# The first MLP product's tile pool, claimed in another order, so that the pieces of w_up lie over the turned input of the convolution and attention's last outputs

## The chip, the cores and the metric

The kernel runs on one core of one Trainium2 chip. The metric is the time on the device in microseconds (us): one launch computes the whole layer. TensorE is called PE, its weight loads PEld, VectorE DVE, ScalarE ACT, GpSimd POOL and SyncE SP, as in the profile. SP does no arithmetic here: it issues most of the DMAs, in one queue, in the order of the program.

## The reference

One layer of a hybrid decoder trunk, for 2048 positions of width 1024, everything in float32:

```python
h = rms_norm(x, attn_norm_g)
z = h @ w_in                                  # q, k, v, gate_b, gate_c, xc
y_attn = swa_sink_attention(q, k, v, sinks)   # window 128, 8 heads of 64, 2 kv heads
y_conv = gate_b * short_conv(gate_c * xc, conv_w)
y = concat(rms_norm(y_attn, attn_out_g), rms_norm(y_conv, conv_out_g))
x = x + y @ w_out
hm = rms_norm(x, mlp_norm_g)
x = x + square(relu(hm @ w_up)) @ w_down      # w_up 1024 x 4096, w_down 4096 x 1024
```

## The kernel before, in words

**Three products for one.** Every float32 operand is split into a high and a low part of a shorter kind, and each product is made as three matmuls of 128x512: high by high, high by low, low by high. The split is two instructions: ACT casts the high part (L397 for blocks of x and of w_down, L416 for pieces of w_up), DVE subtracts it from the original to get the low part (L398, L417). The two products of the MLP are also done with seven block products in the place of eight, numbered 1 to 7; so operands are sums of blocks, and each block product `p` has its own x operand and its own w operand.

**Stages.** The positions go in four chunks of 512 through the mixers (attention and convolution, with the output projection). The last thing that the mixers do is the second half of the last chunk's output projection: matmuls into tiles `pout` from attention's outputs `at` and the weights `w_wo01`, a sum into the row tiles `x1` on DVE (L906), and a store of each of the four row tiles to `x1_dram`, issued by POOL (L913). The matmuls of the MLP's first product (tile `u`, L1421) begin in between: the operands of product 1 are made early (`wu_first0` to `wu_first3`), the others by the MLP's own code. The second product (tile `d`, L1528) comes at the end.

**The first product's loop.** `seq` lists (column group `n`, product `p`). At the start it is product 1 of groups 0 to 3, product 2 of groups 0 to 3, then products 6, 5, 7 of groups 0 to 2, then 3 and 4. Some steps ahead of its matmuls each operand is fetched: a piece of w_up is a tile of 128x512 in tag `w` (names `wu0_12` for group 0, block row 1, column 2; loaded by SP, L411), with 17 buffers; it is split into one of four `wop` tiles (L416 on ACT, L417 on DVE). The x operands `op_x0_p_0` and `op_x0_p_1` are loaded by SP from scratch in DRAM (L396) and split in place (L397, L398). Sums of pieces are made on DVE (L1136 to L1143). Beside the matmuls, `prepare_rest` brings the last 512 rows of x back from `x1_dram` in four tiles `xt_m3_0` to `xt_m3_3` (SP, L1219), and takes their squares on ACT (L275).

**What sets the order.** The code names the engine of every instruction; the framework's scheduler orders the instructions of each engine from the order of the code, priorities and its own costs, and adds the semaphore waits. A tile pool is a stretch of the on-chip memory SBUF; inside it every tag gets its place in the order in which the tags are first used. The MLP's pool opens where the mixers' pool was closed, at the same address, with waits by tile: whoever first writes a new tile waits for the last use of just those old tiles that lie under it. The few `memset` instructions on POOL of one column, with names that end in `_first`, write a first tile of a tag and so claim its place.

The mixers' pool holds, from its start: the row tiles `z` (0 to 12 KB per partition), two buffers `raw` (12 to 28 KB; in the last chunk they hold weights of the output projection, `w_wo11` and then `w_wo01`), five buffers `at` (28 to 48 KB, attention's outputs), `h0` (48 to 64 KB) and `h1` (64 to 80 KB). The last two hold the turned, normed input of the chunk, which the convolution's and the attention's projections read, and after that the blocks of x for the MLP (`xm0`, `xm1`) on their way to DRAM.

## Time and profile before

| | |
|---|---|
| time, median of 3 runs (lowest, highest) | 1934.71 us (1933.54, 1935.15) |
| the profiled execution's own time | 1934.5 us |
| its span, first to last instruction | 1932.8 us |
| PE busy | 1913.2 us, 99% of the span |
| DVE, ACT, POOL busy | 62%, 43%, 14% |
| DMA, mean over the span | 214 GB/s |
| first MLP product (u) | 2688 matmuls, 611.7 us busy |
| second MLP product (d) | 2688 matmuls, 609.4 us busy |

A PE that is busy for 99% of the span leaves some 20 us of gaps in all. Whatever is done on other engines shows in the time only where it opens or closes one of those gaps, or changes the clock that PE is granted.

### The profile page before, as it was taken

To read this page: it belongs to the slowest core of one execution; us is meant where nothing else is said; L and a number is where in the kernel's file an instruction comes from. 1 tells how busy PE (TensorE), PEld (TensorE's weight loads), DVE (VectorE), ACT (ScalarE), POOL (GpSimd) and SP (SyncE) were. 2 spreads that over 40 slices of the span, in tenths; PEclk is the share of its full clock that TensorE was granted. 3 is DMA by queue.
4 is the path that set the end of the run, shared out by engine and by line. 5 is a ranking of instruction groups with operands and counts; after the bars stand their busy time and mean duration, and the time that the engine had idled before them with its cause. 6 is when DMAs were issued, how large, how long until landed. Compare 5 with 4: busy or idle time off the path is not lost.

```text
span 1932.8 us, 24559 instructions
## 1 busy us (share of the span) xinstructions
PE 1913.2 (99%) x8923; PEld 1589.5 (82%) x8923; DVE 1204.1 (62%) x1848; ACT 830.8 (43%) x1565; POOL 275.9 (14%) x474
## 2 busy tenths in 40 slices
PE   8999999999999989999999999999999999999999
PEld 7888888888888778888888888888888888888887
DVE  4886657447456768989877766766534334448541
ACT  5564435335344437444565554554422233232320
POOL 1122212302221112223201110101000000100000
PEclk9999999999999999999999999999999999999999
DMA  9884854464463888777665544537964457766631
GB/s 295 321 306 135 312 211 175 187 249 153 193 267 140 264 282 283 232 235 245 209 233 195 181 162 138 169 124 294 378 211 152 142 164 228 264 228 223 206 135 55
DMA packets 232792, 414.32 MB, mean 214 GB/s; under 512 B 51672, under 2 KB 136160, under 8 KB 219872
## 3 DMA queue, kind: packets, MB, share of 16 engines
q1 hardware_dynamic: 203840, 336.98, 51.8%
q0 software_dynamic: 15424, 51.40, 6.8%
q10 hardware_dynamic: 13408, 24.39, 3.3%
q8 instruction: 70, 1.15, 0.2%
q14 instruction: 50, 0.41, 0.1%
HBM read 286.87 MB, written 125.83 MB: 214 GB/s over the span
## 4 chain that ended last, share of the span: by engine, by line
PE 93%; DMA 2%; DVE 2%; issue 1%; POOL 1%; ACT 1%; SPq 0%; ACTq 0%; POOLq 0%; DVEq 0%
PE d L1528 32%; PE u L1421 31%; PE pout L266 2%; PE pout L268 2%; PE pout L267 2%; PE pz L266 2%; PE pz L267 2%; PE pz L268 2%; PE psc_b L679 2%; PE pc_c L266 2%; PE px_c L266 2%; PE px_c L267 2%; PE pc_c L267 2%; PE pc_c L268 2%; PE px_c L268 2%; PE pb_c L267 1%
## 5 line engine op out<-in xcount | busy, mean ns | idle before, releaser
L1421 PE MATMUL u<-op_x,wop 128*128 128x512 f32 x2688 | 611.7, 390 | 4.6 <-ACT wop L416 4.6
L1528 PE MATMUL d<-op_w,op_f 128*128 128x512 f32 x2688 | 609.4, 389 | 0.0
L1421 PEld LDWEIGHTS u<-op_x,wop 128*128 128x128 f32 x2688 | 505.4, 188 | 110.3 <-ACT wop L416 5.2
L1528 PEld LDWEIGHTS d<-op_w,op_f 128*128 128x128 f32 x2688 | 504.5, 188 | 104.8
L398 DVE TENSOR_TENSOR op_f<-op_f 128x1024 fp32r<-128x1024 f32 x112 | 136.9, 1225 | 234.0 <-ACT op_f L397 233.6
L397 ACT CAST op_f<-op_f 128x1024 fp32r<-128x1024 f32 x112 | 117.5, 1050 | 353.3 <-DMA op_f<-fop 350.2
L416 ACT CAST wop<-wu 128x512 fp32r<-128x512 f32 x156 | 96.2, 620 | 89.9 <-PE u L1421 82.4
L417 DVE TENSOR_TENSOR wop<-wu,wop 128x512 fp32r<-128x512 f32 x156 | 110.6, 710 | 32.6 <-ACT wop L416 17.3
L1157 POOL DMA_DIRECT2D fop<-s x96 | 52.2, 543 | 440.5 <-DVE s L1160 436.3
L1163 DVE TENSOR_TENSOR u<-u,u 128x512 f32<-128x512 f32 x128 | 87.7, 685 | 22.1 <-PE u L1421 22.0
L398 DVE TENSOR_TENSOR op_w<-raw,op_w 128x1024 fp32r<-128x1024 f32 x56 | 68.4, 1222 | 26.3 <-ACT op_w L397 26.2
L397 ACT CAST op_w<-raw 128x1024 fp32r<-128x1024 f32 x56 | 58.8, 1053 | 44.9 <-PE d L1528 22.6
L1169 ACT ACTIVATE u<-u 128x512 f32<-128x512 f32 x64 | 40.5, 632 | 62.9 <-DVE u L1163 61.0
L696 ACT ACTIVATE sc_b<-sc_b,ngm_b 128x128 f32<-128x128 f32 x128 | 49.6, 389 | 25.6 <-DVE ngm_b L693 25.6
L728 POOL TENSOR_SCALAR_AFFINE_SELECT pp_b<-pp_b 128x512 fp32r<-128x512 f32 x60 | 39.8, 675 | 112.8 <-ACT pp_b L721 59.2
L1370 POOL DMA_DIRECT2D wds<-raw x16 | 8.6, 536 | 328.1 <-DVE raw L1368 328.1
L416 ACT CAST wop<-wu_s 128x512 fp32r<-128x512 f32 x64 | 39.6, 620 | 32.2 <-PE u L1421 26.1
L417 DVE TENSOR_TENSOR wop<-wu_s,wop 128x512 fp32r<-128x512 f32 x64 | 45.0, 702 | 12.4 <-ACT wop L416 12.1
L266 PE MATMUL pout<-w_wo,yt_c 128*128 128x512 f32 x128 | 52.5, 410 | 0.0
L268 PE MATMUL pout<-w_wo,yt_c 128*128 128x512 f32 x128 | 52.1, 407 | 0.0
L267 PE MATMUL pout<-w_wo,yt_c 128*128 128x512 f32 x128 | 51.2, 400 | 0.0
L266 PE MATMUL pout<-w_wo,at_b 128*128 128x512 f32 x128 | 50.2, 395 | 0.0
(256 smaller groups left out, 3109.4 us busy)
## 6 DMA issues: line engine op xcount, KB each, us to landing
op_f<-fop SPq DMA_DIRECT2D x112, 512.0 KB, 4.3
raw<-in_w_down_dram SPq DMA_DIRECT2D x72, 512.0 KB, 4.3
wu<-in_w_up_dram SPq DMA_DIRECT2D x128, 256.0 KB, 4.1
w_wo<-wo SPq DMA_DIRECT2D x24, 1024.0 KB, 6.8
fop<-s POOLq DMA_DIRECT2D x96, 256.0 KB, 2.5
fop<-u ACTq DMA_DIRECT2D x64, 256.0 KB, 2.9
op_x<-xop SPq DMA_DIRECT2D x28, 512.0 KB, 6.4
w_q<-q SPq DMA_DIRECT2D x12, 1024.0 KB, 6.2
```

What stands on the lines that cost most here:

```text
L266: nc.tensor.matmul(ps, st(0), mv(0), start=first, stop=False)
L267: nc.tensor.matmul(ps, st(0), mv(1), start=False, stop=False)
L268: nc.tensor.matmul(ps, st(1), mv(0), start=False, stop=last)
L397: nc.scalar.copy(op[:, 0], raw)
L398: nc.vector.tensor_tensor(op[:, 1], raw, op[:, 0].bitcast(F32), op=ALU.subtract)
L416: splits.append(nc.scalar.copy(hi, blk).ins)
L417: nc.vector.tensor_tensor(lo, blk, hi.bitcast(F32), op=ALU.subtract)
L696: nc.scalar.activation(sc[:, hd, :], sc[:, hd, :], AF.Exp, bias=ngm[:, hd : hd + 1], accum_out=den[:, hd : hd + 1])
L1157: eng.dma_start(fop_dram[tb][ORDER_DOWN.index(i)][n // 2][:, n % 2], b)
L1163: return nc.vector.tensor_tensor(dst, ps, b, op=ALU.add).ins
L1421: nc.tensor.matmul(pt, wops[i][:, a, k, :], xops[tb, p][k // 2][:, b, k % 2, :], start=p not in GOES_ON and k + j == 0, stop=k + j == NB + ...
L1528: nc.tensor.matmul(ps[tb][j], fs[tb][:, a, k, j * P : (j + 1) * P], w[:, b, k, :], start=first and p not in GOES_ON and k + n == 0, stop=l ...
```

## The change

```diff
-    for tag in ("f12", "s1", "s2", "s4", "u4", "f11", "w"):
+    for tag in ("u2", "f11", "f12", "s1", "s2", "s4", "u4", "st"):
         nc.gpsimd.memset(piece(tag, f"{tag}_first")[:, :1], 0.0)
+    nc.gpsimd.memset(pool.tile([P, D], F32, tag="xt", name="xt_m_first", bufs=2)[:, :1], 0.0)
+    nc.gpsimd.memset(piece("w", "w_first")[:, :1], 0.0)
```

No tile changes its size or its number of buffers. The order of the claims changes, and with it the place of each tag, counted from the pool's start in KB per partition:

| place | mixers' tile that lies there | MLP's tags before | MLP's tags after |
|---|---|---|---|
| 0 to 12 | z | f12, s1, s2, s4, part of u4 | u2, f11, part of f12 |
| 12 to 28 | raw (w_wo01, the projection's last weights) | u4, f11, 5 of the w | f12, s1, s2, s4, u4, 2 of the st |
| 28 to 48 | at (attention's last outputs) | 10 of the w | 3 of the st, xt, 3 of the w |
| 48 to 64 | h0 | 2 of the w, u2, 3 of the st | 8 of the w |
| 64 to 80 | h1 | 2 of the st, xt | 6 of the w |

So 14 of the 17 pieces of w_up now lie over `h0` and `h1`, where 15 lay over `raw` and `at`; the tiles `xt` for the last rows of x lie over `at`, where they lay over `h1`. Of the 13 pieces that SP loads first, 12 now take places of `h0` and `h1`; the thirteenth, `wu1_12`, lies over the fifth buffer of `at`, which the last chunk no longer uses.

The order of PE's, ACT's and DVE's instructions stays as it was. POOL gets three more memsets, and SP's queue changes in two places. The first is on SP at the end of the mixers, from the last weights of the output projection on. In brackets stand the semaphores that a DMA waits for: PE_49 and the like are counts of an engine's instructions, DMASW counts the landings of POOL's DMAs, DMAHW those of earlier DMAs. Before:

```order
L235 DMA w_wo013_1_6733<-wo01_1_2240 128x2048 [waits DMAHW1_49]
L396 DMA op_x0_2_0_6821<-xop0_1_77 128x1024 [waits DMAHW2_49,PE_49]
L396 DMA op_x0_2_1_6825<-xop0_1_77 128x1024 [waits DMAHW3_49,PE_49]
L1219 DMA xt_m3_0_7369<-x1_dram_75 128x1024 [waits DMAHW4_49,DMASW1_49]
L396 DMA op_x0_6_0_6829<-xop0_2_78 128x1024 [waits DMAHW5_49,Pool_49]
L396 DMA op_x0_6_1_6833<-xop0_2_78 128x1024 [waits DMAHW7_49,DMAHW6_49,DVE_49]
L411 DMA wu0_12_6839<-in_w_up_dram 128x4x128
L411 DMA wu1_12_6841<-in_w_up_dram 128x4x128 [waits DMAHW1_49,DMAHW0_49,PE_49]
L411 DMA wu2_12_6843<-in_w_up_dram 128x4x128
L411 DMA wu3_12_6845<-in_w_up_dram 128x4x128 [waits DMAHW2_49]
```

Now:

```order
L235 DMA w_wo013_1_6733<-wo01_1_2240 128x2048 [waits DMAHW1_49]
L396 DMA op_x0_2_0_6827<-xop0_1_77 128x1024 [waits DMAHW2_49,PE_49]
L396 DMA op_x0_2_1_6831<-xop0_1_77 128x1024 [waits DMAHW3_49,PE_49]
L396 DMA op_x0_6_0_6835<-xop0_2_78 128x1024 [waits DMAHW4_49,Pool_49]
L396 DMA op_x0_6_1_6839<-xop0_2_78 128x1024 [waits DMAHW5_49]
L411 DMA wu0_12_6845<-in_w_up_dram 128x4x128 [waits DMAHW6_49]
L411 DMA wu1_12_6847<-in_w_up_dram 128x4x128 [waits DMAHW7_49]
L411 DMA wu2_12_6849<-in_w_up_dram 128x4x128 [waits DMAHW0_49]
L411 DMA wu3_12_6851<-in_w_up_dram 128x4x128 [waits DMAHW1_49]
```

The load of `xt_m3_0`, which waits for the landing of POOL's first store to `x1_dram` (DMASW1), has left this place, and the wait of `wu1_12` for PE is gone; that one was for the last L267 of the output projection, into `pout3_0_1_3`. A second wait for PE further on, of `wu2_22` for the projection's very last matmul, is gone as well. The wait of `op_x0_6_0` for POOL stays; it is for the last mask of attention.

The second place is on SP too, some 25 loads later, where the pieces for groups 3 and 4 are loaded as earlier ones become free. Before:

```order
L411 DMA wu4_11_7230<-in_w_up_dram 128x4x128 [waits DMAHW7_49,DVE_49]
L1219 DMA xt_m3_1_7393<-x1_dram_75 128x1024 [waits DMAHW0_49]
L411 DMA wu4_21_7282<-in_w_up_dram 128x4x128 [waits DMAHW1_49,DVE_49]
L411 DMA wu4_22_7284<-in_w_up_dram 128x4x128 [waits DMAHW2_49,DVE_49]
L1219 DMA xt_m3_2_7422<-x1_dram_75 128x1024 [waits DMAHW3_49,Activation_49]
```

Now:

```order
L411 DMA wu4_11_7236<-in_w_up_dram 128x4x128 [waits DMAHW6_49,DVE_49]
L1221 DMA xt_m3_0_7375<-x1_dram_75 128x1024 [waits DMAHW7_49,PE_49]
L411 DMA wu4_21_7288<-in_w_up_dram 128x4x128 [waits DMAHW0_49,DVE_49]
L1221 DMA xt_m3_1_7399<-x1_dram_75 128x1024 [waits DMAHW1_49,PE_49]
L411 DMA wu4_22_7290<-in_w_up_dram 128x4x128 [waits DMAHW2_49,DVE_49]
L1221 DMA xt_m3_2_7428<-x1_dram_75 128x1024 [waits DMAHW7_49,DMAHW3_49,Activation_49]
```

`xt_m3_0` comes in here, and `xt_m3_1` falls back behind `wu4_21`, which waits for DVE to have made the low part of product 7 of group 0 (`wop_0_7`). Their waits for PE are for matmuls of the output projection.

On POOL the memsets stand behind the four stores of `x1`, as they did. Before:

```order
L913 DMA x1_dram_75<-x1_3_3_6228 128x1024
L1105 MEMSET f12_first_6805 128x1
L1105 MEMSET s1_first_6807 128x1
L1105 MEMSET s2_first_6809 128x1
L1105 MEMSET s4_first_6811 128x1
L1105 MEMSET u4_first_6813 128x1
L1105 MEMSET f11_first_6815 128x1
L1105 MEMSET w_first_6817 128x1
L1394 MEMSET op_first_6819 128x1
```

Now:

```order
L913 DMA x1_dram_75<-x1_3_3_6228 128x1024
L1105 MEMSET u2_first_6805 128x1
L1105 MEMSET f11_first_6807 128x1
L1105 MEMSET f12_first_6809 128x1
L1105 MEMSET s1_first_6811 128x1
L1105 MEMSET s2_first_6813 128x1
L1105 MEMSET s4_first_6815 128x1
L1105 MEMSET u4_first_6817 128x1
L1105 MEMSET st_first_6819 128x1
L1106 MEMSET xt_m_first_6821 128x1
L1107 MEMSET w_first_6823 128x1
L1396 MEMSET op_first_6825 128x1
```

Where the first product hands over to the second, the pool of the second lies over the first's, and a few waits change: the loads of w_down into `raw` (L1359) wait for the last splits of pieces of w_up, where they waited for the last stores of `u2` and of `wds`.

## The prediction

> **What bounds the kernel now.** I read the page first, then PE's waits, then the time around the one long wait, engine by engine. On the page, three lines:

> ```profile
> PE 1913.2 (99%) x8923; PEld 1589.5 (82%) x8923; DVE 1204.1 (62%) x1848; ACT 830.8 (43%) x1565; POOL 275.9 (14%) x474
> PE   8999999999999989999999999999999999999999
> L1421 PE MATMUL u<-op_x,wop 128*128 128x512 f32 x2688 | 611.7, 390 | 4.6 <-ACT wop L416 4.6
> L1528 PE MATMUL d<-op_w,op_f 128*128 128x512 f32 x2688 | 609.4, 389 | 0.0
> ```

> PE is the bound in all 40 slices; only the first slice and the fifteenth (676 to 725 us) are an 8. A change of layout cannot make matmuls fewer, so it can only touch gaps. The second MLP product has no idle time at all, the first has 4.6 us, all before one instruction, and the list of PE's waits has it at the top:

> ```profile
> PE u L1421 <- ACT wop L416: 4.6, 1, 4.6
> ```

> The timeline of PE shows its place; the rows of the table of windows below it have the window and its length, PE's busy time and matmuls, the granted clock, the DMA share and GB/s:

> ```profile
> 709.47 5.15 PE L1421 MATMUL u<-op_x,wop 128*128 128x512 f32 x22
> 719.20 41.04 PE L1421 MATMUL u<-op_x,wop 128*128 128x512 f32 x173 [4.58 <-ACT wop L416]
> 714.70:719.20 4.50, 0.01 (x1) 0.99 1.08 377
> 719.20:724.00 4.80, 4.80 (x14) 0.66 1.15 345
> 724.00:729.00 5.00, 5.00 (x23) 1.00 1.10 357
> ```

> PE ends product 1 of the first groups at 714.62, stands for 4.58 us, and then runs its next 4.8 us at a mean clock of 0.66. The change lies on this spot.

> **What holds the operand up.** PE waits for `wop_0_2`. The timelines of SP, ACT and DVE tell why it is late:

> ```profile
> 689.79 0.97 SPq L235 DMA_DIRECT2D w_wo<-wo  x2
> 692.66 0.80 SPq L396 DMA_DIRECT2D op_x<-xop  x2
> 706.05 0.32 SPq L1219 DMA_DIRECT2D xt_m<-x_dram  x1
> 706.46 0.86 SPq L396 DMA_DIRECT2D op_x<-xop  x2
> 707.37 16.64 SPq L411 DMA_DIRECT2D wu<-in_w_up_dram  x13
> 703.02 0.64 POOL L913 DMA_DIRECT2D x_dram<-x  x1 [7.89 <-DVE x L906]
> 713.70 1.05 ACT L397 CAST op_x<-op_x 128x1024 fp32r<-128x1024 f32 x1 [10.32 <-DMA op_x<-xop]
> 718.52 1.27 ACT L416 CAST wop<-wu 128x512 fp32r<-128x512 f32 x2 [1.46 <-DMA wu<-in_w_up_dram]
> 709.67 0.75 DVE L906 SCALAR_TENSOR_TENSOR x<-pout,ra,x 128x512 f32<-128x512 f32 x1 [1.97 <-PE pout L268]
> 714.78 1.23 DVE L398 TENSOR_TENSOR op_x<-op_x 128x1024 fp32r<-128x1024 f32 x1 [4.36 <-ACT op_x L397]
> 719.17 1.35 DVE L417 TENSOR_TENSOR wop<-wu,wop 128x512 fp32r<-128x512 f32 x2 [0.85 <-ACT wop L416]
> ```

> From 693.46 to 706.05, 12.6 us, SP's queue issues nothing: at its head stands `xt_m3_0`, which waits for POOL's store of 703.02 to land. Behind it stand `op_x0_6` and all 13 pieces of w_up. Then `wu1_12` waits once more, for the output projection's end. ACT gets `op_x0_6_0` at 713.70 and `wu0_12` at 718.52. DMA was not the limit while SP stood:

> ```profile
> 695.00:700.00 5.00, 5.00 (x24) 4.14 (x23) 0.75 (x1) 0.00 (x0) 0.13 (x1) 1.00 0.96 353
> 700.00:705.00 5.00, 5.00 (x24) 4.14 (x23) 3.04 (x4) 3.08 (x4) 0.64 (x1) 1.00 0.20 80
> ```

> The last column falls from 353 GB/s to 80 there, against 377 in the stall.

> **The change, part by part.** *Removed: both waits at the head of SP's queue.* `op_x0_6` now waits only for a mask of attention, which was made before the projection's last half, so it follows `op_x0_2` at 693.46 (13.0 us earlier), and `wu0_12` after another 0.86 us at 694.3. When do they land? The nearest rows are the DMA answers for the same two loads before (last column: us to landing, first for `op_x0_6_0`, then for `wu0_12`), and the longest landing of an x operand between 690 and 745 us:

> ```profile
> op_x<-xop SPq DMA_DIRECT2D x1, 512.0 KB, 7.2
> wu<-in_w_up_dram SPq DMA_DIRECT2D x1, 256.0 KB, 11.1
> DMA to landing us min/median/max: 5.8/8.5/12.9
> ```

> So `op_x0_6_0` lands at 700.7, at most 706.4; `wu0_12` at 705.4, at most 707.2. I take about 704 and 706, since both stand behind w_wo and `op_x0_2`.

> *What is late next.* The order on DVE is unchanged: after the sum at 709.67 come two L398 for `op_x0_6`, then L417 for `wop_0_2`. With the data there, DVE goes through: 709.67 + 0.75 + 2 x 1.23 + 0.69 = 713.57 at most. PE wants `wop_0_2` at 714.62, so 1.05 us are left. ACT has cast by then: from 704, two casts of 1.05 and one of 0.62 give some 707. `wop_1_2` follows on DVE 0.69 later and is wanted 12 matmuls later; the pace is (5.15 - 0.39)/21 = 0.227 us, so 2.7 us later. The stall of 4.58 goes, whole. Between the ends: nothing of it goes if the data come as late as now, and no more than 4.58 can.

> *The clock.* The window 719.20 to 724.00 lost (1 - 0.66) x 4.80 = 1.63 us. By its count of matmuls (14, where the next 5.0 us have 23, so 22 for 4.8) it would be 8 x 0.227 = 1.8 us. The slow stretch begins as the stall ends, and no other stretch around it is below 0.99; I take it as the stall's and count 1.63, with 0 and 1.8 as ends. [...]

> *Moved: the loads of the last rows of x.* `xt_m3_0` now stands behind `wu4_11`, where `xt_m3_1` stood, and `xt_m3_1` behind `wu4_21`. On ACT their squares are in the same place in the order:

> ```profile
> 741.25 0.50 SPq L1219 DMA_DIRECT2D xt_m<-x_dram  x1
> 743.17 2.71 SPq L411 DMA_DIRECT2D wu<-in_w_up_dram  x2
> 746.07 1.05 ACT L275 ACTIVATE junk_m<-xt_m 128x1024 bf16<-128x1024 f32 x1
> 747.25 1.06 ACT L275 ACTIVATE junk_m<-xt_m 128x1024 bf16<-128x1024 f32 x1
> 750.24 1.37 ACT L416 CAST wop<-wu 128x512 fp32r<-128x512 f32 x2 [1.84 <-DVE wu L1143]
> 751.87 1.28 DVE L417 TENSOR_TENSOR wop<-wu,wop 128x512 fp32r<-128x512 f32 x2
> DMA to landing us min/median/max: 3.3/4.2/4.3
> ```

> In the times of before: `xt_m3_0` issued at 741.25 lands at 745.5 (the last row is for these four loads), wanted at 746.07. `xt_m3_1`, behind one of the two loads of 743.17 (1.36 us), lands at 744.5 + 4.2 = 748.7, wanted at 747.25: ACT waits 1.5 us. Its next instruction idles 1.84 us for DVE anyway, so that hides it. Without that cover there is more: those casts are for `wop_0_3`, which is ready at 751.87 + 0.69 = 752.6 and wanted after 156 matmuls of the restart, 719.20 + 1.63 + 156 x 0.227 = 756.2; 3.6 us. Cost 0; ends 0 and 4.7 (a rival, below).

> *SP's further queue.* The five loads from `op_x0_5` on come earlier too; those of `op_x0_3` wait for POOL's stores, which land as before. They are wanted 84 matmuls after the restart, 19 us, and were in time with a queue that ran 13 us later. PE goes only 6.2 us earlier, so their slack grows.

> *POOL's memsets.* Three more, behind the four stores as before.

> ```profile
> 711.27 0.17 POOL L1105 MEMSET s_first<- 128x1 f32 x3
> ```

> Three take 0.17 us. On SP only `op_x0_4_1` waits for the last of POOL's memsets, and it is wanted 168 matmuls after the restart: 0.

> *The hand-over to the second product.* There SP's queue waits for PE itself:

> ```profile
> 1299.06 26.25 SPq L396 DMA_DIRECT2D op_f<-fop  x4
> 1325.47 2.03 SPq L1359 DMA_DIRECT2D raw<-in_w_down_dram  x4
> 1311.63 0.68 DVE L417 TENSOR_TENSOR wop<-wu,wop 128x512 fp32r<-128x512 f32 x1
> ```

> The loads into `raw` at 1325.47 stand behind a load that waits for the second product's first matmuls. Their new wait, the last L417, is over at 1312.3, 13 us before. Cost 0, gain 0.

> **The sum.** 4.58 + 1.63 = 6.2 us. The profiled execution took 1934.5 us, 1.7 more than its span and 0.2 below the median of 1934.71: 1934.5 - 6.2 = **1928.3 us**. The runs shown lie 1.6 us apart, so about 0.2% (3.9 us) is what a measurement can tell from no change; 6.2 is 0.32%.

> **Rivals.**

> *A rest of the stall stays.* At the new place the pieces share the DMA engines with POOL's four stores of 512 KB: 4 x 0.52 MB at 357 GB/s are 5.9 us. If `op_x0_6` took the longest landing, 12.9, and all of those 5.9 on top, it would be there at 693.5 + 18.8 = 712.3; two casts of 1.05 and one of 0.62 bring `wop_0_2`'s high part to 715.0, and DVE's two of 1.23, each behind its cast (the second from 714.6), and one of 0.69 its low part to 716.5: a stall of 1.9 us. With the clock counted as kept that is 1930.2. For it: `wu0_12` took 11.1 us where stores were under way. Against: the DMA engines are at 80 GB/s just then. [...]

> *The last rows of x come too late.* If `xt_m3_1` took the 12.9 us, it would land at 744.5 + 12.9 = 757.4, ACT would wait 10.2 us; 1.84 and 3.6 are covered, 4.7 reach PE, and with it perhaps the clock's 1.6: 1934.5 - 6.2 + 4.7 to 6.3 = 1933.0 to 1934.6, no change. For it: the queue is busier around the start. Against: 4.3 us is the longest that these loads took.

> *Slower: the output projection starves.* The weights `w_wo01` were issued from 689.79 on, the second half some 0.5 us later:

> ```profile
> w_wo<-wo SPq DMA_DIRECT2D x2, 1024.0 KB, 8.4
> 700.10 1.05 ACT L397 CAST op_x<-op_x 128x1024 fp32r<-128x1024 f32 x1 [6.74 <-DMA op_x<-xop]
> 699.27 0.39 PE L267 MATMUL pout<-w_wo,at_b 128*128 128x512 f32 x1
> ```

> The second half lands at 698.7, and PE first reads it at 699.27: 0.6 us. Now 15 loads (4.4 MB) queue behind from 693.5. If the engines shared their rate among all that is queued, w_wo could come up to 4.4/0.353 = 12.5 us later (the 353 GB/s of 695 to 700 us); PE would stand some 12 us at 699 and lose 1.6 of clock: 1934.5 - 6.2 + 13.5 = 1941.8. It decides from a landing 5.2 us later on, where stall and clock eat the gain. Against: `op_x0_2`, 2.4 us behind w_wo in the same queue, was cast from 700.10 on, after w_wo's landing: the queue served them in turn.

> *The change does nothing.* If the freed places still had to wait, 1934.5. Against: the program has no wait for PE left on the first 13 pieces.

> **How the numbers follow.** The stall and its clock go whole: 0.80. A rest stays: 0.08. Rows of x too late: 0.06. Starved projection: 0.04. Nothing: 0.02. The first two are faster by over 0.2% (1930.2 is 4.5 below the median): 0.88. Same: 0.06 + 0.02 = 0.08. Slower: 0.04. The range takes in the first two: from 1928.3 less the runs' 1.2 below the median and the clock's other 0.2, 1926.9, up to 1930.2 plus the 0.4 by which the highest run lies above the median, rounded up to 1930.8.

> **What would show it.** Right: PE's waits have no line from `u` to `wop` L416; the table around 714 to 724 us shows PE full at clock 1.00; SP issues `op_x0_6` near 693.5 and has all 13 pieces out by some 712; the first product ends 6 us earlier, and nothing after it is shorter. Wrong: a new wait of PE on `pout` near 699, on `wop` near 714 or near 750, or the old gap in its place.

## The result, and the profile after

The changed kernel took **1927.43 us** (median of 7 runs, 1924.23 to 1932.66), the kernel before 1934.71 us (median of 7 runs beside it, 1933.54 to 1938.19). The ratio is 0.9963, with a 95% interval of 0.9949 to 0.9976: 7.2 us less, between 4.6 and 9.9. Two more sessions gave 0.9963 (0.9950 to 0.9977) and 0.9963 (0.9950 to 0.9975). The profiled execution took 1928.92 us, with a span of 1927.1.

The page of the changed kernel, and the top of its list of PE's waits:

```profile
PE 1912.4 (99%) x8923; PEld 1589.7 (82%) x8923; DVE 1204.2 (62%) x1848; ACT 830.5 (43%) x1565; POOL 270.4 (14%) x477
PE   8999999999999999999999999999999999999999
PE ptq_b L652 <- DVE z L641: 3.4, 1, 3.4
```

The 8 in the fifteenth slice is gone, and so is the line of `u` and `wop`. What tops the list now is a wait in the first mixer, which the kernel before had as well (3.0 us). The timelines of SP, ACT, DVE and PE around the place of the change:

```profile
690.56 0.97 SPq L235 DMA_DIRECT2D w_wo<-wo  x2
693.45 1.76 SPq L396 DMA_DIRECT2D op_x<-xop  x4
695.26 18.10 SPq L411 DMA_DIRECT2D wu<-in_w_up_dram  x13
713.46 6.62 SPq L396 DMA_DIRECT2D op_x<-xop  x8
704.33 2.01 ACT L397 CAST op_x<-op_x 128x1024 fp32r<-128x1024 f32 x2
706.23 1.14 ACT L416 CAST wop<-wu 128x512 fp32r<-128x512 f32 x2
710.46 0.75 DVE L906 SCALAR_TENSOR_TENSOR x<-pout,ra,x 128x512 f32<-128x512 f32 x1 [1.97 <-PE pout L268]
711.12 2.35 DVE L398 TENSOR_TENSOR op_x<-op_x 128x1024 fp32r<-128x1024 f32 x2
713.39 1.89 DVE L417 TENSOR_TENSOR wop<-wu,wop 128x512 fp32r<-128x512 f32 x3
700.05 0.39 PE L267 MATMUL pout<-w_wo,at_b 128*128 128x512 f32 x1
710.25 64.99 PE L1423 MATMUL u<-op_x,wop 128*128 128x512 f32 x286
1313.64 8.55 PE L1530 MATMUL d<-op_w,op_f 128*128 128x512 f32 x37
```

SP issues all four x operands in one go and the 13 pieces right behind them. ACT casts `wop_0_2` at 706, where it was 718.5. DVE, freed by PE's last `pout` at 710.46, goes through its two L398 and its three L417 without a pause. PE runs from 710.25 on with no idle time in front of any row. The same stretches of the table of windows (PE's busy time and matmuls, granted clock, DMA share, GB/s):

```profile
714.70:719.20 4.50, 4.50 (x22) 1.00 1.11 384
719.20:724.00 4.80, 4.80 (x23) 1.00 1.03 415
724.00:729.00 5.00, 5.00 (x24) 1.00 1.03 419
```

Before, PE was busy for 0.01 us in the first of these and ran the second at 0.66. For the gain at the spot itself, the row that starts the second product in the kernel before:

```profile
1319.36 2.88 PE L1528 MATMUL d<-op_w,op_f 128*128 128x512 f32 x12
```

From the first `u` behind the projection to the first `d` are 1319.36 - 709.47 = 609.89 us before and 1313.64 - 710.25 = 603.39 after: **6.50 us** less.

### The profile page after: what moved, and what is told of

It reads as the page before. It is cut to its first block, busy times and chain, and to the rows that moved or that the text cites. A ratio compares the mean times of both kernels' runs of the same rounds, so it can differ in the third digit from the quotient of the medians.

```text
span 1927.1 us, 24567 instructions
## 1 busy us (share of the span) xinstructions
PE 1912.4 (99%) x8923; PEld 1589.7 (82%) x8923; DVE 1204.2 (62%) x1848; ACT 830.5 (43%) x1565; POOL 270.4 (14%) x477
## 3 DMA queue, kind: packets, MB, share of 16 engines
q8 instruction: 70, 1.15, 0.2%
## 4 chain that ended last, share of the span: by engine, by line
PE 94%; DMA 2%; DVE 1%; SPq 1%; POOL 1%; ACT 1%; issue 0%; ACTq 0%; DVEq 0%; POOLq 0%
PE d L1530 32%; PE u L1423 32%; PE pout L266 3%; PE pout L268 3%; PE pout L267 3%; PE pz L266 2%; PE pz L267 2%; PE pz L268 2%; PE psc_b L679 2%; PE pc_c L266 2%; PE pc_c L267 2%; PE pc_c L268 2%; PE px_c L266 2%; PE px_c L268 2%; PE px_c L267 2%; PE pb_c L267 1%
## 5 line engine op out<-in xcount | busy, mean ns | idle before, releaser
L1530 PE MATMUL d<-op_w,op_f 128*128 128x512 f32 x2688 | 609.4, 389 | 0.0
L398 DVE TENSOR_TENSOR op_f<-op_f 128x1024 fp32r<-128x1024 f32 x112 | 136.9, 1225 | 234.9 <-ACT op_f L397 234.6
L397 ACT CAST op_f<-op_f 128x1024 fp32r<-128x1024 f32 x112 | 117.6, 1051 | 353.5 <-DMA op_f<-fop 350.4
L416 ACT CAST wop<-wu 128x512 fp32r<-128x512 f32 x156 | 96.1, 620 | 88.8 <-PE u L1423 85.2
L417 DVE TENSOR_TENSOR wop<-wu,wop 128x512 fp32r<-128x512 f32 x156 | 111.7, 718 | 32.3 <-ACT wop L416 19.6
L398 DVE TENSOR_TENSOR op_w<-raw,op_w 128x1024 fp32r<-128x1024 f32 x56 | 68.4, 1222 | 25.5 <-ACT op_w L397 25.4
L397 ACT CAST op_w<-raw 128x1024 fp32r<-128x1024 f32 x56 | 58.8, 1052 | 44.7 <-PE d L1530 22.7
L416 ACT CAST wop<-wu_s 128x512 fp32r<-128x512 f32 x64 | 39.7, 621 | 33.6 <-PE u L1423 28.3
L417 DVE TENSOR_TENSOR wop<-wu_s,wop 128x512 fp32r<-128x512 f32 x64 | 44.7, 699 | 12.5 <-ACT wop L416 12.4
L268 PE MATMUL pout<-w_wo,yt_c 128*128 128x512 f32 x128 | 52.1, 407 | 0.0
L267 PE MATMUL pout<-w_wo,yt_c 128*128 128x512 f32 x128 | 51.2, 400 | 0.0
## 6 DMA issues: line engine op xcount, KB each, us to landing
op_f<-fop SPq DMA_DIRECT2D x112, 512.0 KB, 4.4
raw<-in_w_down_dram SPq DMA_DIRECT2D x72, 512.0 KB, 4.2
wu<-in_w_up_dram SPq DMA_DIRECT2D x128, 256.0 KB, 4.1
w_wo<-wo SPq DMA_DIRECT2D x24, 1024.0 KB, 6.8
fop<-s POOLq DMA_DIRECT2D x96, 256.0 KB, 2.6
fop<-u ACTq DMA_DIRECT2D x64, 256.0 KB, 2.8
op_x<-xop SPq DMA_DIRECT2D x28, 512.0 KB, 6.6
w_q<-q SPq DMA_DIRECT2D x12, 1024.0 KB, 6.3
```

The lines of the kernel that those rows point to most:

```text
L267: nc.tensor.matmul(ps, st(0), mv(1), start=False, stop=False)
L268: nc.tensor.matmul(ps, st(1), mv(0), start=False, stop=last)
L397: nc.scalar.copy(op[:, 0], raw)
L398: nc.vector.tensor_tensor(op[:, 1], raw, op[:, 0].bitcast(F32), op=ALU.subtract)
L416: splits.append(nc.scalar.copy(hi, blk).ins)
L417: nc.vector.tensor_tensor(lo, blk, hi.bitcast(F32), op=ALU.subtract)
```

## The experiments

Every kernel of this section was timed beside the kernel before. `e0_changed` is the changed kernel again, as a base:

> The changed kernel once more, beside the experiments on the same chip, as the base for them. Expected: 1926 to 1929 us, 6 to 8 us under the kernel before; no wait of PE for wop at u0_2; a stretch at half clock behind the wait for z at 47 us in some of its runs.

It took 1927.64 us (5 runs, 1926.78 to 1929.22) against 1934.48 of the kernel before (27 runs). Its profile, the second of the changed kernel, has no wait of PE for `wop` either.

**Rows of x back over the turned input.** Only the claim of the tag `xt` is taken out of the changed kernel:

```diff
-    nc.gpsimd.memset(pool.tile([P, D], F32, tag="xt", name="xt_m_first", bufs=2)[:, :1], 0.0)
```

> The changed kernel without the new memset of the tag xt: the rows of x go back over the convolution's turned input, as in the kernel before, and the pieces of w_up stay off the rows of x1. So xt_m3_0 is at the head of SP's queue again, in front of op_x0_6, and wu1_12 still does not wait for the projection's last matmul. If the wait in SP's queue was the cost (my theory): SP stands idle again from about 693.5 to 706 us, PE waits 4.0 to 4.6 us for wop_0_2, the clock behind it falls to about 0.66 again, and the time is 1933.9 to 1935 us. If the place of the pieces of w_up, and their own wait for PE, was the cost (the rival): the wait of PE is under 1 us and the time is 1927 to 1929 us.

It took 1934.38 us (11 runs), ratio to the kernel before 0.9997 (0.9988 to 1.0006). Its SP queue, its PE and its windows:

```profile
692.30 0.81 SPq L396 DMA_DIRECT2D op_x<-xop  x2
705.70 0.32 SPq L1220 DMA_DIRECT2D xt_m<-x_dram  x1
706.11 0.86 SPq L396 DMA_DIRECT2D op_x<-xop  x2
718.90 7.38 PE L1422 MATMUL u<-op_x,wop 128*128 128x512 f32 x24 [4.64 <-ACT wop L416]
719.20:724.00 4.80, 4.80 (x15) 0.64 1.15 345
```

SP stands from 693.1 to 705.7 again, PE waits 4.64 us, the clock falls to 0.64, and all of the gain is gone, although most pieces of w_up still lie over `h0` and `h1`. The edit is not quite clean: without the 8 KB of `xt` ahead of them the pieces move 8 KB down, so that 10 of the 17 lie over `h0` and `h1` and 7 over `at` (14 and 3 in the changed kernel), and `wu1_12` waits for PE again. But SP comes to that wait only at 708.0, behind `xt_m3_0`, and finds it over: it goes on at once. With `xt_m3_0` at the queue's head the place of the pieces is worth nothing. The rival falls.

**The load moved, the layout left.** The kernel before, with `xt_m3_0` ordered behind the piece `wu4_11`:

```diff
+        up_loads[n, i, k] = nc.sync.dma_start(pieces(b), src).ins
...
-            nc.sync.dma_start(xt, x1_dram[r : r + P, :])
+            with nullcontext() if t else tc.issue_after(up_loads[4, 1, 1]):
+                nc.sync.dma_start(xt, x1_dram[r : r + P, :])
```

> The kernel before, with its old pool layout, and one edit: the load of xt_m3_0 is issued behind the load of the piece wu4_11, where the changed kernel has it. wu1_12 keeps its wait for the projection's last matmul (until about 709.4 us). If the wait of xt_m3_0 in SP's queue was the cost (my theory): op_x0_6 is issued at about 693.5 us, PE's wait for wop_0_2 is gone, and a rest of 0 to 1.5 us may stand before u1_2, whose wop_1_2 is wanted at 717.3 us and whose piece cannot be issued before 709.4; time 1928 to 1930 us. If the new layout itself was needed (the rival): PE still waits over 4 us and the time is 1934 to 1935 us.

It took 1929.84 us (11 runs), ratio 0.9979 (0.9970 to 0.9987): 4.6 us of the gain, with the old layout. The wait at 714 us is gone. The rest of the wait is there, but not where I had put it. SP, ACT, PE and windows of this kernel (the second row is the last 12 of the 13 pieces, the third the longest wait of SP's queue there):

```profile
693.70 25.72 SPq L412 DMA_DIRECT2D wu<-in_w_up_dram  x13
708.42 11.00 SPq L412 DMA_DIRECT2D wu<-in_w_up_dram  x12
SPq L412 <- PE pout L268: 11.0, 1, 11.0
719.52 6.31 SPq L396 DMA_DIRECT2D op_x<-xop  x8
727.19 1.06 ACT L397 CAST op_x<-op_x 128x1024 fp32r<-128x1024 f32 x1 [4.22 <-DMA op_x<-xop]
731.27 0.73 PE L1424 MATMUL u<-op_x,wop 128*128 128x512 f32 x2 [1.35 <-ACT wop L417]
732.50 12.79 PE L1424 MATMUL u<-op_x,wop 128*128 128x512 f32 x48 [0.49 <-DVE wop L418]
714.60:719.20 4.60, 4.60 (x22) 1.00 0.98 293
732.50:736.10 3.60, 3.60 (x9) 0.53 1.05 406
```

`wu1_12` itself was in time. But the 13 pieces take SP 25.7 us where the changed kernel takes 18.1; in this layout two of them, `wu1_12` and `wu2_22`, wait for PE. The trace parts the two: SP issues `wu0_12` at 693.70 and then stands until 708.42 at `wu1_12`, the last 11 us of it for the projection's matmuls, while the wait of `wu2_22` is over when SP comes to it. The other 12 pieces then take 11.0 us, so the stand of 14 us makes the whole row only 7.6 us longer. So the next x operands start at 719.52 and not at 713.46, ACT waits 4.22 us for one of them, the casts behind it are late, and PE stands 1.35 and 0.49 us at 730 to 732.5, again with slow matmuls behind. So the old place of the pieces has a price as well, which the wait of `xt_m3_0` hid (in the kernel before `wu1_12` held SP only from 708.6 to 709.4). Its size is less sure than its cause: the medians are 2.2 us apart (1929.84 against 1927.64) with intervals that overlap, and in the profiles the stretch from the first `u` behind the projection to the first `d` is 4.3 us longer (607.71 against 603.39).

**The gap filled with idle work.** The kernel before, with 16 matmuls (`SPIN_UP`) into a bank that nobody reads, just before `u0_2`; `last_mm` is PE's last matmul before them:

```diff
+        if (n, p) == (0, 2):
+            idle = bank("tr", "idle_up")
+            with tc.issue_after(last_mm):
+                for _ in range(SPIN_UP):
+                    last_mm = nc.tensor.matmul(
+                        idle, xops[0, 1][0][:, 0, 0, 0, :P], xops[0, 1][1][:, 0, 0, :, :], start=True, stop=True,
+                        skip_group_check=True,
+                    ).ins
```

> The kernel before, with 16 extra matmuls of 128x512 between u3_1 and u0_2, into a PSUM bank that nobody reads; all other orders are as before. They take 16 x 0.227 = 3.6 us of the 4.58 us that PE stood idle. If the half clock behind the wait comes from PE's standing idle (my theory): u0_2 starts where it started, about 1 us of idle time is left, the granted clock in the 5 us behind it is 0.95 to 1.00 and not 0.66, and the time falls by 1.6 to 2.0 us, to 1932.7 to 1933.1. If the slow stretch has another cause than the idle time (the rival): the clock behind it is 0.66 again and the time is within 0.4 us of the kernel before.

It took 1933.54 us (11 runs), ratio 0.9994 (0.9985 to 1.0003). PE and windows:

```profile
714.84 3.79 PE L1424 MATMUL idle_up<-op_x,op_x 128*128 128x512 f32 x16
719.53 2.80 PE L1430 MATMUL u<-op_x,wop 128*128 128x512 f32 x10 [0.91 <-ACT wop L417]
719.20:724.00 4.80, 4.47 (x19) 1.00 1.15 346
724.00:729.00 5.00, 5.00 (x24) 1.00 1.12 341
```

The clock answers the question: `u0_2` starts as late as before, yet the granted clock behind the gap is 1.00 and not 0.66. DMA is as busy there as before (345 and 346 GB/s), so the half clock came from PE's standing. The time does not answer it: 0.9 us less, and the interval takes in 1.7 as well as nothing. In the profiled execution the stretch to the first `d` was 0.6 us shorter than before and not 1.7; the trace has waits of PE of 0.1 to 0.4 us near 720, 880 and 1310 us that the kernel before did not have in its own. At the spot itself, with the small waits near 720 counted, it gained 1.4 us. The waits near 880 and 1310 are not the idle matmuls' doing: the second profile of the changed kernel has the like at 877 and 1307 us, the first has none.

**The wait in the first mixer.** What tops the changed kernel's list is open to another change. In a first version the transposes of block 0 (`ptq_b`) are ordered behind 18 of the convolution's matmuls (`conv_mm` holds every third of these, `PTQ` is 5):

```diff
-            for j in range(4):
-                nc.tensor.transpose(pt[:, j * P : (j + 1) * P], zt[:, j * P : (j + 1) * P], ident)
+            with nullcontext() if b else tc.issue_after(conv_mm[PTQ]):
+                for j in range(4):
+                    nc.tensor.transpose(pt[:, j * P : (j + 1) * P], zt[:, j * P : (j + 1) * P], ident)
```

> The changed kernel, with one more edit in its first mixer: the transposes of block 0's queries and keys (ptq_b, ptk_b), for which PE stood 2.2 to 3.4 us at 44 to 47 us with a half-clock stretch behind it, come behind 18 of the convolution's matmuls, not among the first ones. If PE is then free to run on (first theory): no wait for z, no half clock, px_c starts at about 55 us and not at 58.8 to 61, and the time is 1921 to 1924.5 us. If DVE is next (second theory, which I take): the split of w_wx stands in DVE's order behind the chain of z and is done only from about 58 us on, so that PE waits 2 to 3.1 us there, with a half clock behind it: 1925.5 to 1928.5 us, nothing gained against the changed kernel's 1927.6.

It took 1927.43 us (5 runs, 1926.74 to 1928.48): nothing against the changed kernel, as the second theory had it. Its trace does not show the wait that the theory names. In that execution PE waited 1.2 us for its first rows of x, its clock rose only at 11.0 us (5.6 in the changed kernel's profile), and the convolution began at 45.8 us and not at 43.1; so PE came to `px_c` at 57.35, when DVE had just got to the split of `w_wx`:

```profile
57.05 2.50 DVE L247 TENSOR_TENSOR w_wx<-raw_wx,w_wx 128x512 fp32r<-128x512 f32 x4
```

The late start hid the wait here; that the five times have the same reason is not shown, as only one of them has a trace. The next version orders DVE too, and has 21 matmuls ahead of the transposes (`PTQ` is 6):

```diff
-        with ahead(7):
+        with tc.high_priority(offset=150) if name == "wx0" and not c else ahead(7):
...
+            with tc.issue_after(qk_after[b]) if b in qk_after else nullcontext():
                 nc.vector.tensor_tensor(zqk, zqk, rq[:, :, None].to_broadcast([P, nh, DH]), op=ALU.mult)
```

Here `qk_after` holds the last split of `w_wx` for block 1, and the last split of block 0's keys for block 2.

> As the run before it, with 21 matmuls ahead of the transposes, and with DVE's order in that stretch changed: the split of w_wx ahead of z_1's products, the split of block 0's queries and keys ahead of z_2's products. If the place of w_wx's split in DVE's queue is what makes PE wait next (the theory taken): px_c starts at about 55 us with no wait over 0.5 us from 43 to 75 us, the granted clock stays at 1.00 there, and the time is 1921 to 1924.5 us, 3 to 6 us under the changed kernel. If a later chain takes it back (the rival: scores waiting for DVE, or a fixed chain of the mixers behind it): the wait shows behind 60 us, and the time is 1925.5 to 1928.5 us.

It took 1925.54 us (5 runs, 1922.79 to 1926.51), ratio to the kernel before 0.9949 (0.9936 to 0.9963). Its split of `w_wx`, its `px_c` and two windows (all engines: PE, PEld, DVE, ACT, POOL, then clock, DMA share, GB/s):

```profile
51.93 2.59 DVE L247 TENSOR_TENSOR w_wx<-raw_wx,w_wx 128x512 fp32r<-128x512 f32 x4 [2.64 <-DMA qkv<-w_qkv]
54.77 0.39 PE L271 MATMUL px_c<-h_a,w_wx 128*128 128x512 f32 x1
44.00:47.00 3.00, 3.00 (x15) 2.47 (x14) 2.10 (x4) 0.00 (x0) 1.26 (x2) 1.00 1.08 372
47.00:50.00 3.00, 3.00 (x17) 2.50 (x16) 1.69 (x4) 2.30 (x5) 2.23 (x2) 1.00 1.00 409
```

There is no wait and no half clock from 43 to 75 us: with DVE's order changed as well, PE gets to `px_c` at 54.77 and goes on. The split begins at 51.93, where it began at 57.05 in the run before and at 57.45 in the changed kernel; an estimate from these rows is that with the old order PE would have stood over 2 us for it at this pace. Yet the median lies at the lower edge of the rival's range. The changed kernel and this version were run once more, side by side:

> The changed kernel again, run beside the next one on one chip, so that the two are compared in one session: 1926 to 1929 us, with one or two windows of half clock behind the wait at 47 us in those runs whose first loads land early.

> The kernel e5_q_and_dve again, for an interval against the changed kernel. If its gain is real (the theory): 1.5 to 4 us under the changed kernel's median of the same session, with no half clock before 75 us. If the 2.1 us of the first session were a session's luck (the rival): within 0.8 us of the changed kernel.

They took 1926.97 us (1925.85 to 1927.60) and 1925.12 us (1922.90 to 1925.64), 5 runs each. Side by side this version is the faster one by 1.85 us, and its slowest run is below the fastest of the changed kernel; the 2.1 us of 1925.54 against 1927.64 are between two sessions. In their profiles the changed kernel waits 3.1 us for `z` with one piece of half clock behind it, and this version has neither, as forecast. The theory's mechanism is in the trace, but its size is not in the medians: it forecast 3 to 6 us. The spans of the profiled executions differ by 3.7 and 4.0 us; the other runs have no trace that would say where half of it stays.

## Why the prediction was right, step by step

**The stall** (4.58 us). Right in its cause, and close in size. The experiments part the two waits that it named: with `xt_m3_0` back at the queue's head the stall is 4.64 us, with it away the stall at 714 us is gone, with the old layout too. That the pieces' old place has a price of its own, some 2 us by the medians, was not in the prediction; it named `wu1_12`'s wait only as a part of the same stall.

**The clock** (1.63 us, at most 1.8). The mechanism is shown by the filled gap: with 0.91 us of standing just ahead of `u0_2`, where there had been 4.58, the granted clock behind it was 1.00 and not 0.66. The size: counted by the starts of the matmuls, the first one behind the stall comes 4.74 us later than in the changed kernel, and the next eight lose another 1.67 us; that is 6.41 of the 6.50 us measured at the spot, where the sum had 4.58 + 1.63 = 6.2, and the other 0.09 us are lost in small waits near 1316 us. (The trace of before records half clock for 3.413 us from 719.09, of which PE works 3.30.) The 1930.2 of the rival with a rest of 1.9 us counts the clock as kept. No run shows that: in the kernel with the load moved 1.84 us of standing, in two pieces, were followed by 3.4 us at half clock (0.53 over the 3.6 us from 732.5). Had the rival come true, it could have cost up to 1.7 us more than 1930.2, an estimate: half of those 3.4 us.

**What is late next.** DVE's splits came as said: `wop_0_2` is done by 713.39 + 0.69 = 714.1, wanted at 710.25 + 5.15 = 715.4; the slack is 1.3 us, where 1.05 stood. `op_x0_6` was there for the cast at 704.33 and `wu0_12` by 706.23, against "about 704 and 706"; the 13 pieces were out by 713.4, where "some 712" was forecast. PE did not wait for `pout` at 700, so the starved projection is out.

**The last rows of x.** The wait of ACT for `xt_m3_1` is there and hidden, as forecast, but shorter, 0.87 us where I had 1.5:

```profile
735.02 0.47 SPq L1221 DMA_DIRECT2D xt_m<-x_dram  x1
737.40 0.46 SPq L1221 DMA_DIRECT2D xt_m<-x_dram  x1
742.46 1.06 ACT L275 ACTIVATE junk_m<-xt_m 128x1024 bf16<-128x1024 f32 x1 [0.87 <-DMA xt_m<-x_dram]
744.02 0.62 ACT L416 CAST wop<-wu 128x512 fp32r<-128x512 f32 x1 [0.41 <-DVE wu L1145]
```

**The hand-over.** Nothing behind the first `d` changed in length: it begins 5.72 us earlier than before and so does the last `d`.

**What the sum left out.** The profiled execution gained 5.6 us and not 6.5, because it came to the projection's end 0.78 us later (710.25 against 709.47), for reasons that lie ahead of the change. It left the first mixer's stretch below 1.5 us later, and short waits of PE between 660 and 674 us, of which the kernel before had the longest (1.76 us), gave half of that back. The windows in the first mixer, before and then after (PE's busy time and matmuls, clock, DMA share, GB/s):

```profile
47.00:50.40 3.40, 3.29 (x11) 0.55 1.02 412
50.40:53.80 3.40, 3.40 (x16) 1.00 1.05 435
```

```profile
47.00:50.40 3.40, 2.89 (x10) 0.50 1.02 408
50.40:53.80 3.40, 3.40 (x10) 0.56 1.04 430
```

The wait for `z` there was 3.0 us before and 3.4 after, and the half clock behind it twice as long. That is a matter of the run, not of the kernel: the changed kernel's second profile waits 2.2 us and has one stretch of 3.4 us, and the kernel without the claim of `xt` had neither wait nor half clock in its own, as PE waited 1.3 us for its first rows of x there, had full clock only from 12.6 us on and began the convolution 3.7 us later.

So it is partly luck that the median came within 0.9 us of the forecast. The medians' gains in the three sessions are 7.3, 6.8 and 6.9 us, each with an interval of about 2.5 us to either side; what they have beyond the 6.5 of the spot is not shown by the profiles.

## What to carry to other kernels

A new tile layout is read best by the waits that it puts into an in-order DMA queue: one load that waits at the head holds back every load behind it (15 loads for 12.6 us here), whatever their own places are free for, and a second wait shows only when the first is gone (`wu1_12` held SP for 0.8 us behind `xt_m3_0`, and for 14 us with that load moved). Price a stall of PE with the clock that follows it (4.58 us and 1.63 here). When a gap is closed early in a kernel, look at once at the next engine's order, since the next operand's split may be queued where the gap used to cover it.

## What was not expected of the hardware

Behind nine of the ten waits of PE in the table below the granted clock fell to one half, for 3.4 us or for twice that: up to the last matmul the clock records of the trace of before have two such pieces, each of 3.413 us, those of the changed kernel one of 6.827 us. In these records the pieces lie on a grid. Before, they start at 46.66 and 719.09 us; the 672.43 us between them are 197 times 3.413 us to within 0.1 us. The first full clock is recorded from 5.70 us, 40.96 us ahead of the first piece, which is 12 times 3.413; in the changed kernel it is recorded from 5.57 us, and the piece starts at 46.53, again 40.96 us later. How long PE stood idle did not set their length in a simple way: 3.4 us at 44 us in the changed kernel had 6.8 us of half clock behind them, 4.58 us at 714.6 before had 3.4. The third column lays PE's idle time on the grid: what falls into the stretch of 3.413 us just before the half clock (with no half clock, into the fullest stretch), and into the next one:

| kernel, place | idle time of PE | of it in one stretch, in the next | half clock behind it |
|---|---|---|---|
| before, 668.5 us | 1.76 us | 1.76, 0.57 | none |
| load moved, 730 us | 1.35 and 0.49 us | 1.84, 0 | 3.4 us |
| changed, second profile, 44 us | 2.2 us | 2.15, 0.02 | 3.4 us |
| load moved, 44 us | 2.7 us | 2.17, 0.57 | 3.4 us |
| before, 44 us | 3.0 us | 2.56, 0.45 | 3.4 us |
| changed, third profile, 44 us | 3.1 us | 2.50, 0.62 | 3.4 us |
| changed, 44 us | 3.4 us | 2.45, 0.98 | 6.8 us |
| gap filled, 44 us | 3.4 us | 2.23, 1.20 | 6.8 us |
| before, 714.6 us | 4.58 us | 3.41, 0.11 | 3.4 us |
| rows of x back, 714.3 us | 4.64 us | 3.11, 0 | 3.4 us |
